# A two-layer decoder trunk on one core: squares, sums and transpositions of the feed-forward parts are placed anew, and the second output weights are prepared at another place

## The chip, the core and the metric

The kernel runs on one core of one Trainium2 chip. The core has five engines with instruction streams of their own: TensorE (PE, matrix products), VectorE (DVE), ScalarE (ACT), GpSimd (POOL) and SyncE (SP), which here only issues DMAs. Each engine works its stream off in order and waits where an operand of its next instruction is not ready. The metric is the device time of one execution in microseconds (us), the median of several runs.

## The reference

The input x is 1024 tokens by 1024 features, in float32. Two layers follow each other. A layer is a token mixer and a dense part, each with a residual and a LayerNorm:

```python
for i in range(DEPTH):                       # DEPTH = 2, ALPHA = 4 ** 0.25
    if i % 2 == 0:
        m = _mla(x, ...)                     # latent attention, 8 heads, ends in o @ w_o
    else:
        m = _diff_attn(x, ...)               # differential attention, 8 heads, RMS norm, ends in o @ w_o
    x = _layernorm(ALPHA * x + m, ln_mix_g[i], ln_mix_b[i])
    x = _layernorm(ALPHA * x + jnp.square(jax.nn.relu(x @ w_up)) @ w_down, ln_ffn_g[i], ln_ffn_b[i])
```

`w_up` is 1024 x 4096, `w_down` 4096 x 1024. Everything is float32, and the result is held to float32 closeness.

## The kernel before

**Numbers as pairs.** A float32 operand of a large product is scaled by a factor, cut into an upper and a lower float16 half, and multiplied in three float16 products (helper `mm3`, L185). ACT makes the upper half (L264), DVE the lower (L265). The factor comes from the root of a sum of squares: ACT squares rows with an accumulator, DVE sums (L269 turns the sum to bf16), PE adds over the partitions with a product of ones (L274, results called `tot_...`), and DVE and ACT make the root.

**Layers and names.** Names that end in A (or have A before a number) belong to the first layer, with B to the second. A layer runs in this order: mixer by heads, output projection `o @ w_o` with residual and LayerNorm by tiles of 128 tokens (`o_steps`: `scan` squares the rows of the o weights, `weights` halves them, `tile_steps` does a tile), the up projection, the down projection with the last LayerNorm. In the trace: latent attention 100 to 380 us, its output projection to 515, up A to 806, down A to 1128, a prologue of the differential attention to 1160, that attention to 1580, its output projection to 1705, up B to 1998, down B to the end at 2310.

**Up projection.** It goes by 16 groups g of features in a scheme of seven products for eight (`u_p1` to `u_p7`, 12 products of 128 x 512 each, into `ab`, `c`, `d`). ACT copies the first result out of PSUM with its scale into `pu` (L1039); this frees the PSUM tile `ab` for the products on `xT2`. The relu-squares go through GpSimd sums `hs` (L1094 to L1097) to a DRAM scratch `hs_d`. Beside it `wd_scan(g)` loads two 512 KB blocks of the down weights (`wds`, L1121, issued by SP) and squares them on ACT (L1122). The rows come from a ring of eight (tag `X`), which the results of the up projection share.

**Down projection.** Seven products m of eight steps st, 24 matrix products a step, on operands `h16` (read back from `hs_d` as `hr`) and `w16`, made by ACT and DVE some three steps ahead (`d_operands`). Its factors come from `down_scale`: key "A" for the first seven column sums, made in group 14; key "B" for all eight, made after step (0,2). At m = 5 the tiles 0 to 3 are finished (`fin_stats`, `fin_rstd`, `fin_apply`, L1229 to L250), and after m = 6 the tiles 4 to 7, tile by tile. In the first layer `to_xt` transposes each finished tile on PE (`tp_n`, L216) into the halves `xt_n`, on which the next layer's projections `qkv` run.

**Order.** Inside `in_order()` blocks (the up and down loops, the prologue of the differential attention) the engines follow the text of the program. Elsewhere a list scheduler moves instructions as buffers and operands allow. The fillers of an attention (`diff_filler`) hand it pieces of other work, each with a weight, to be put between score tiles. DMAs leave SP's queue in its order. The prologue re-reads tiles 6 and 7 of the first layer's result from DRAM (`x1_d`), transposes them and projects four token pairs of head 0 (`qkv0_0`, ...).

## Time and profile before

| what | value |
|---|---|
| median of 3 runs | 2301.41 us (2296.93 to 2302.53) |
| the profiled execution | 2311.53 us |
| its span in the trace | 2309.8 us |
| mean granted TensorE clock | 0.969 of full |
| PE busy | 2136.2 us, 92% of the span |
| DVE busy | 1684.8 us, 73% |
| ACT busy | 1300.7 us, 56% |
| POOL busy | 529.1 us, 23% |

The profiled execution is 10.1 us longer than the median of the runs that were only timed. A granted clock of 1 stands for 2.4 GHz, one of 0.5 for 1.2 GHz. PE's busy time counts slow products at their full length, so a stall costs its idle time and, where the clock falls behind it, half of the slow stretch as well.

### The profile page before, as it was taken

The page shows a single profiled execution, that of the slowest core. Times are in us where ns is not written, and L with a number is a line of the kernel's source. Part 1 is how long each engine was busy: PE and PEld are TensorE (multiplying, and loading weights), DVE is VectorE, ACT ScalarE, POOL GpSimd, SP SyncE. Part 2 cuts the span into 40 slices and gives each one's busy share as a digit, 9 for nine tenths or more (in the row PEclk, how much of TensorE's full clock was granted, in tenths as well). Part 3 has the DMA queues.
Part 4 walks back from the last instruction along what each step waited for, and adds up shares of the span by engine and source line. Part 5 has one row for each costly group of instructions (what it writes and reads, how often), then busy time and mean ns, then how long its engine had stood idle before and what let it go on. Part 6 is the DMA issues. An engine that isn't in the chain of part 4 may idle for free. (4 is left out here: it accounts for less than half of the span.)

```text
span 2309.8 us, 31741 instructions
## 1 busy us (share of the span) xinstructions
PE 2136.2 (92%) x11255; PEld 1191.6 (52%) x11255; DVE 1684.8 (73%) x2951; ACT 1300.7 (56%) x2400; POOL 529.1 (23%) x381
## 2 busy tenths in 40 slices
PE   7999898989999899999699999969989999999997
PEld 7878775444444344444356655644444444444443
DVE  5677675767777579877578888784857776588787
ACT  5465664446666355446388777673455665354443
POOL 1101001816666310000000001000826666300000
PEclk9999999989999999999899999988989999999999
DMA  4154767526666776652565565455436666856641
GB/s 146 33 104 91 147 123 188 194 101 205 207 213 207 264 281 218 201 192 82 160 155 126 126 122 106 84 118 150 162 142 205 209 210 223 326 198 210 218 155 55
DMA packets 454831, 384.29 MB, mean 166 GB/s; under 512 B 251376, under 2 KB 346624, under 8 KB 454672
## 3 DMA queue, kind: packets, MB, share of 16 engines
q1 hardware_dynamic: 452736, 376.51, 55.2%
q0 software_dynamic: 1936, 5.75, 0.9%
q8 instruction: 88, 1.44, 0.3%
q14 instruction: 71, 0.58, 0.1%
HBM read 247.97 MB, written 83.89 MB: 144 GB/s over the span
## 5 line engine op out<-in xcount | busy, mean ns | idle before, releaser
L185 PE MATMUL yA<-w16A,h16A 128*128 128x512 f16 x1344 | 294.9, 382 | 4.4 <-DVE X2A L1229 3.1
L185 PE MATMUL yB<-w16B,h16B 128*128 128x512 f16 x1344 | 292.8, 380 | 4.6 <-DVE X2B L1229 3.1
L185 PE MATMUL qkv<-wqkv,xt_nA 128*128 128x384 f16 x1536 | 268.5, 328 | 1.0 <-DVE wqkv L265 0.7
L185 PEld LDWEIGHTS <-wuB 128*128 128x128 f16 x1344 | 132.1, 99 | 172.0 <-issue 18.1
L185 PEld LDWEIGHTS <-wuA 128*128 128x128 f16 x1344 | 132.2, 99 | 170.9 <-issue 16.0
L185 PEld LDWEIGHTS <-h16A 128*128 128x128 f16 x1344 | 132.2, 98 | 167.3 <-issue 12.5
L185 PEld LDWEIGHTS <-h16B 128*128 128x128 f16 x1344 | 131.8, 98 | 168.1 <-issue 11.4
L185 PEld LDWEIGHTS <-xt_nA 128*128 128x128 f16 x1536 | 150.0, 99 | 95.8 <-issue 4.4
L1585 DVE TENSOR_REDUCE nmx_d<-ds 128x2 f32<-128x256 f32 (+5 forms) x96 | 90.1, 951 | 24.0 <-PE ds L413 23.6
L265 DVE SCALAR_TENSOR_TENSOR h16B<-hrB,SCB,h16B 128x1024 f16<-128x1024 f32 x56 | 73.3, 1308 | 37.8 <-ACT h16B L264 37.2
L265 DVE SCALAR_TENSOR_TENSOR h16A<-hrA,SCA,h16A 128x1024 f16<-128x1024 f32 x56 | 73.8, 1317 | 35.5 <-ACT h16A L264 35.4
L264 ACT ACTIVATE h16A<-hrA,SCA 128x1024 f16<-128x1024 f32 x56 | 63.9, 1141 | 61.0 <-issue 47.9
L264 ACT ACTIVATE h16B<-hrB,SCB 128x1024 f16<-128x1024 f32 x56 | 63.9, 1140 | 59.9 <-issue 47.9
L413 PE MATMUL s<-kn,qn 128*128 128x512 f32 (+2 forms) x288 | 83.5, 385 | 8.3 <-DVE ph L427 7.8
L185 PE MATMUL oA<-woA,otA 128*128 128x512 f16 x384 | 86.7, 387 | 4.1 <-DVE ph L427 4.1
L185 PE MATMUL oB<-woB,otB 128*128 128x512 f16 x384 | 85.4, 379 | 0.0
L265 DVE SCALAR_TENSOR_TENSOR wuB<-wuB_s,cuB,wuB 128x1024 f16<-128x1024 f32 (+1 forms) x32 | 56.7, 1771 | 34.9 <-ACT wuB L264 34.9
L185 PE MATMUL av_d<-pt16d,dv 128*128 128x256 f16 (+1 forms) x480 | 59.3, 277 | 24.4 <-DMA pt16d<-phd 24.4
L265 DVE SCALAR_TENSOR_TENSOR wuA<-wuA_s,cuA,wuA 128x1024 f16<-128x1024 f32 (+1 forms) x32 | 54.9, 1716 | 34.9 <-ACT wuA L264 34.9
L264 ACT ACTIVATE w16B<-wdB,RBB 128x1024 f16<-128x1024 f32 x40 | 45.7, 1142 | 53.5 <-DVE wdB L1186 53.5
L264 ACT ACTIVATE w16A<-wdA,RBA 128x1024 f16<-128x1024 f32 x40 | 45.7, 1141 | 53.4 <-DVE wdA L1186 53.4
L1489 POOL MEMSET ones_f<- 128x128 f32 x1 | 0.2, 205 | 305.3 <-PE yA L185 305.3
(876 smaller groups left out, 5099.1 us busy)
## 6 DMA issues: line engine op xcount, KB each, us to landing
hrA<-hs_d SPq DMA_DIRECT2D x56, 512.0 KB, 3.8
hrB<-hs_d SPq DMA_DIRECT2D x56, 512.0 KB, 3.8
wuA_r<-in_ffn_w_up_dram SPq DMA_DIRECT2D x32, 512.0 KB, 4.5
wdsA<-in_ffn_w_down_dram SPq DMA_DIRECT2D x32, 512.0 KB, 6.5
wdA<-in_ffn_w_down_dram SPq DMA_DIRECT2D x32, 512.0 KB, 4.7
wuB_r<-in_ffn_w_up_dram SPq DMA_DIRECT2D x32, 512.0 KB, 4.3
wdsB<-in_ffn_w_down_dram SPq DMA_DIRECT2D x32, 512.0 KB, 5.9
wdB<-in_ffn_w_down_dram SPq DMA_DIRECT2D x32, 512.0 KB, 4.6
```

What stands on the lines that cost most here:

```text
L185: nc.tensor.matmul(dst, l, r, start=first and m == 0, stop=last and m == n - 1, skip_group_check=resumed)
L264: nc.scalar.mul(hi, src, scale)
L265: nc.vector.scalar_tensor_tensor(out=lo, in0=src, scalar=scale, in1=hi, op0=ALU.mult, op1=ALU.subtract)
L413: nc.tensor.matmul(dst, q_, k_(c0 // 512, n), start=m == 0, stop=m == len(pairs) - 1)
L1489: nc.gpsimd.memset(ones_f, 1.0)
L1585: nc.vector.tensor_reduce(out=nmx[:, ms], in_=st["wide"][:, :, :nk] if i < 4 else st[m], axis=AX.X, op=ALU.max, negate=True)
```

## The change

Six things change.

1. The residual is no longer multiplied by ALPHA. The eight GpSimd multiplications a layer in `tile_steps` (L320) and the eight ACT multiplications a layer at step (0,4) of the down projection go. In their place the factor that the product is scaled back with is divided by ALPHA, and the LayerNorm's epsilon by ALPHA squared.
2. The end of `tile_steps` becomes three pieces (sums, squares, root).
3. `wd_scan` is cut in two. `wd_fetch(g + 1)` issues the loads at the start of iteration g, where load and squares stood before; `wd_scan(g + 1)`, now the squares alone, stands after `u_p5(g + 1)`.
4. `down_scale` is cut in two. `down_sum` (DVE's sum and its bf16 copy) stands earlier: before `u_p1` of group 14's iteration, and after step (0,0). `down_scale` keeps the product of ones and the root.
5. In the first layer tiles 0 to 3 are transposed one or two steps later, and tiles 6 and 7 straight from SBUF after their `fin_apply`, not from `x1_d` in the prologue.
6. The second layer's o weights: the text places the squares among the projections of head 6 (`H - 2`) in place of head 7, and part of the halves among head 7's.

```diff
@@ o_steps
             nc.vector.reciprocal(icw, cw)
+            nc.vector.tensor_scalar(out=icw, in0=icw, scalar1=1.0 / ALPHA, scalar2=None, op0=ALU.mult)
...
-                nc.gpsimd.tensor_scalar(out=t["x"], in0=t["x"], scalar1=ALPHA, scalar2=None, op0=ALU.mult)
...
-            def end():
-                nmean = residual(t["y"], icw, t["x"], f"m{nm}{i}")
-                st[i] = t["x"], nmean, ln_stats(t["x"], nmean, t["y"], f"m{nm}{i}")
+            def sums():
+                t["m"] = residual(t["y"], icw, t["x"], f"m{nm}{i}")
+            def squares():
+                t["q"] = ln_ssq(t["x"], t["m"], t["y"], f"m{nm}{i}")
+            def root():
+                st[i] = t["x"], t["m"], rstd_of(t["q"], 1.0 / D, LN_EPS_A, f"ln_m{nm}{i}")
@@ mixer_out_and_ffn
+            def wd_fetch(g):
+                wds[g] = [row(f"wds{nm}{g}{f_}") for f_ in range(2)]
+                for f_ in range(2):
+                    nc.sync.dma_start(out=wds[g][f_], in_=wdn[:, g, f_, :])
             def wd_scan(g):
-                for f_ in range(2):
-                    wr = row(f"wds{nm}{g}{f_}")
-                    nc.sync.dma_start(out=wr, in_=wdn[:, g, f_, :])
+                for f_, wr in enumerate(wds.pop(g)):
                     nc.scalar.activation(wr, wr, AF.Square, accum_out=wdsq[g // 2][...])
...
+            def down_sum(n, key):
+                tsum = fp.tile([P, 1], F32, tag="tsum", name=f"tsum{nm}{key}", bufs=2)
+                nc.vector.tensor_reduce(out=tsum, in_=c1["T"][:, :n], axis=AX.X, op=ALU.add)
+                tb[key] = total_in(tsum, f"cd{nm}{key}")
...
                     if g + 1 < NG:
-                        wd_scan(g + 1)
+                        wd_fetch(g + 1)
+                    if g == NG - 2:
+                        down_sum(NA, "A")
...
                         u_p5(g + 1)
+                        wd_scan(g + 1)
...
-                    if (m, st_) == (0, 4):
-                        for i in range(NT):
-                            nc.scalar.mul(X[i], X[i], ALPHA)
...
+                    if (m, st_) == (0, 0):
+                        down_sum(NS, "B")
                     if (m, st_) == (0, 2):
                         down_scale(NS, "B")
...
-                            if layer == 0 and i > 0:
+                        else:
+                            if layer == 0 and i in (1, 2):
                                 to_xt(xt_n, i - 1, "n", ps_wide)
-                        else:
                             fin_rstd(i)
                             fin_apply(i)
-                    if m == 6 and st_ == 1 and layer == 0:
-                        to_xt(xt_n, 3, "n")
+                    if m == 6 and st_ in (1, 2) and layer == 0:
+                        to_xt(xt_n, 1 + st_, "n")
...
+                if layer == 0:
+                    to_xt(xt_n, 6, "n")
                 fin_apply(7)
+                if layer == 0:
+                    to_xt(xt_n, 7, "n")
@@ diff_filler and prologue
+            if (h, u) in ((H - 2, 0), (H - 2, 2)):
+                steps = merge(steps, [(0.1, lambda k=k: wo_scan(k)) for k in range(2 * u, 2 * u + 4)])
+            if (h, u) == (H - 2, 3):
+                steps.append((0.1, wo_scale))
             if h == H - 1:
-                steps += [(0.1, lambda k=k: wo_scan(k)) for k in range(4 * u, 4 * u + 4)]
+                steps = merge(steps, [(0.1, lambda k=k: wo_load(k)) for k in range(2 * u, 2 * u + 2)])
...
-            xn = [wp.tile([P, D], F32, tag="raw", name=f"x1_{t}", bufs=3) for t in range(2)]
-            for t in range(2):
-                nc.gpsimd.dma_start(out=xn[t], in_=x1_d[(6 + t) * P : (7 + t) * P, :])
```

Four places show how the instructions move. The first is ScalarE in the second layer's up projection, between group 3's last piece and group 4's copy `puB4`; `wdsB40` and `wdsB41` are the two blocks of group 4, `wdsB30` and `wdsB31` those of group 3. Before:

```order
L264 ACTIVATE wuB4_3_16723<-wuB4_s4_16543,cuB4_16651 128x512
L1048 ACTIVATE hB30_16738<-abB1_16219,cuB3_16492 128x512
L1122 ACTIVATE wdsB40_16770,wdsqB4_16769<-wdsB40_16770 128x1024
L1122 ACTIVATE wdsB41_16773,wdsqB4_16769<-wdsB41_16773 128x1024
L1039 ACTIVATE puB4_16790<-abB0_16189,cuB4_16651 128x512
```

Now:

```order
L265 ACTIVATE wuB4_3_16697<-wuB4_s4_16516,cuB4_16625 128x512
L1057 ACTIVATE hB30_16712<-abB1_16195,cuB3_16465 128x512
L1136 ACTIVATE wdsB30_16590,wdsqB2_16566<-wdsB30_16590 128x1024
L1136 ACTIVATE wdsB31_16591,wdsqB2_16566<-wdsB31_16591 128x1024
L1048 ACTIVATE puB4_16763<-abB0_16165,cuB4_16625 128x512
```

The squares keep their place in the stream ahead of `pu`, but they are those of the group before, whose blocks were asked for one iteration earlier.

The second is TensorE after the first layer's last down product: `tp_nA50` to `tp_nA71` are the transpositions of the halves of tiles 5 to 7, and `qkv0_2` is the third projection block of head 0. Before (`x1_0` is the tile re-read from DRAM; tile 7 stands behind `qkv0_2`):

```order
L216 MATMUL tp_nA50_10117<-ident_r_77,X2A5_7920 128x128 x4
L216 MATMUL tp_nA51_10124<-ident_r_77,X2A5_7920 128x128 x4
L216 MATMUL tp_nA60_10260<-ident_r_77,x1_0_10178 128x128 x4
L216 MATMUL tp_nA61_10267<-ident_r_77,x1_0_10178 128x128 x4
L185 LDWEIGHTS xt_nA00_9498
L185 MATMUL qkv0_2_10274<-wqkv00_9846,xt_nA00_9498 128x384
```

Now:

```order
L217 MATMUL tp_nA50_10104<-ident_r_77,X2A5_7918 128x128 x4
L217 MATMUL tp_nA51_10111<-ident_r_77,X2A5_7918 128x128 x4
L217 MATMUL tp_nA60_10139<-ident_r_77,X2A6_7920 128x128 x4
L217 MATMUL tp_nA61_10146<-ident_r_77,X2A6_7920 128x128 x4
L217 MATMUL tp_nA70_10156<-ident_r_77,X2A7_7922 128x128 x4
L217 MATMUL tp_nA71_10163<-ident_r_77,X2A7_7922 128x128 x4
L186 LDWEIGHTS xt_nA00_9520
L186 MATMUL qkv0_2_10271<-wqkv00_9819,xt_nA00_9520 128x384
```

Tiles 6 and 7 come from the tiles `X2A6` and `X2A7` themselves, and both stand ahead of `qkv0_2`.

The third is ScalarE at the end of m = 5 and the start of m = 6 of the first layer's down projection; `woB...s_raw` are the squares of the second layer's o weights. Before, none of them stands here:

```order
L264 ACTIVATE h16A57_9588<-hrA57_9514,SCA_4631 128x1024
L264 ACTIVATE w16A57_9589<-wdA57_9516,RBA_4633 128x1024
L1248 ACTIVATE ljA2_9597,fsq_A2_9596<-X2A2_7914,rsum_fA2_9594 128x1024
L264 ACTIVATE xt_nA00_9498<-tp_nA10_9599,xs_c_1526 128x4x128
L264 ACTIVATE xt_nA01_9499<-tp_nA11_9606,xs_c_1526 128x4x128
L264 ACTIVATE h16A60_9639<-hrA60_9561,SCA_4631 128x1024
L264 ACTIVATE w16A60_9640<-wrA110_8034,RBA_4633 128x1024
```

Now:

```order
L265 ACTIVATE h16A57_9575<-hrA57_9485,SCA_4630 128x1024
L296 ACTIVATE woB1s_raw_14272,fwB_10172<-woB1s_raw_14272,gsub_1521 128x1024
L296 ACTIVATE woB2s_raw_14322,fwB_10172<-woB2s_raw_14322,gsub_1521 128x1024
L265 ACTIVATE w16A57_9576<-wdA57_9487,RBA_4632 128x1024
L296 ACTIVATE woB3s_raw_14339,fwB_10172<-woB3s_raw_14339,gsub_1521 128x1024
L1270 ACTIVATE ljA2_9584,fsq_A2_9583<-X2A2_7912,rsum_fA2_9581 128x1024
L265 ACTIVATE h16A60_9612<-hrA60_9548,SCA_4630 128x1024
L265 ACTIVATE w16A60_9613<-wrA110_8029,RBA_4632 128x1024
L265 ACTIVATE xt_nA00_9520<-tp_nA10_9618,xs_c_1526 128x4x128
L265 ACTIVATE xt_nA01_9521<-tp_nA11_9625,xs_c_1526 128x4x128
L296 ACTIVATE woB4s_raw_14547,fwB_10172<-woB4s_raw_14547,gsub_1521 128x1024
```

All eight squares lie between the halves of steps (5,6) and (6,2): the re-read tiles no longer hold two of the three buffers that the squares need, and the scheduler moves them up to where these are free. Before, they stood in the prologue.

The fourth is ScalarE in the last head. `woB0` to `woB3` are upper halves of o weights, `p_d7_1` and `phd7_0` pieces of the last head's score tiles, `phd6_7` one of the head before. Before:

```order
L1540 CAST dz7_6_15054<-qk7_6_14950 128x2x4x64
L264 ACTIVATE woB0_15134<-woB0w_raw_15132,fwB_10157 128x1024
L264 ACTIVATE woB1_15146<-woB1w_raw_15144,fwB_10157 128x1024
L264 ACTIVATE woB2_15170<-woB2w_raw_15168,fwB_10157 128x1024
L1588 ACTIVATE nmx_d7_1_14754<-nmx_d7_1_14754,w_c_4624 128x2
L426 ACTIVATE phd7_0_14730<-p_d7_0_14713,rec_d7_0_14725 128x128
L1590 ACTIVATE p_d7_1_14756,sume_d7_1_14755<-ds7_1_14757,nmx_d7_1_14754,w_c_4624 128x256
L1590 ACTIVATE ds7_1_14757,sume_d7_1_14755<-ds7_1_14757,nmx_d7_1_14754,w_c_4624 128x256
L264 ACTIVATE woB3_15175<-woB3w_raw_15173,fwB_10157 128x1024
```

Now:

```order
L1619 ACTIVATE ds6_6_1_14591,sume_d6_6_14551<-ds6_6_1_14591,nmx_d6_6_14550,w_c_4623 128x896
L265 ACTIVATE woB0_14876<-woB0w_raw_14874,fwB_10172 128x1024
L265 ACTIVATE woB1_14964<-woB1w_raw_14962,fwB_10172 128x1024
L265 ACTIVATE woB2_14999<-woB2w_raw_14997,fwB_10172 128x1024
L1617 ACTIVATE nmx_d6_7_14620<-nmx_d6_7_14620,w_c_4623 128x1
L1543 ACTIVATE qk7_6_14985<-qkv7_6_14903 128x256
L1569 CAST dz7_4_14847<-qk7_4_14790 128x2x4x64
L1545 ACTIVATE dv7_14476<-qkv7_6_14903 128x128
L1619 ACTIVATE p_d6_7_14622,sume_d6_7_14621<-ds6_7_0_14623,nmx_d6_7_14620,w_c_4623 128x1024
```

The halves now begin at score tile 6 of head 6 and lie beside the last projections (`qkv7_6`, `qkv7_7`); the last two of them stand beside head 7's first and shortest tile, and none behind it.

## Rows read from the trace of the kernel before

**Rows 1.** The span in stretches; columns in the first line, PEclk the granted clock.

```profile
core 0: us, PE busy (x) PEld busy (x) DVE busy (x) ACT busy (x) POOL busy (x), PEclk, DMA share, GB/s
1128.00:1160.00 32.00, 18.12 (x108) 11.61 (x107) 16.50 (x35) 16.02 (x35) 1.11 (x2) 0.73 0.72 218
1705.00:1998.00 293.00, 281.91 (x1298) 126.95 (x1296) 202.65 (x294) 172.25 (x280) 175.43 (x110) 0.99 0.64 218
```

**Rows 2.** Waits of TensorE over the span: total us, times, longest.

```profile
PE abA L185 <- ACT puA L1039: 8.7, 6, 4.4
PE abB L185 <- ACT puB L1039: 8.3, 5, 4.5
PE tot_cdBB L274 <- DVE totb_cdBB L269: 2.8, 1, 2.8
PE tp_nA L216 <- DMA x<-x_d: 13.9, 1, 13.9
PE tp_nA L216 <- DVE X2A L250: 5.7, 3, 3.0
PE ds L413 <- ACT woB L264: 4.5, 1, 4.5
```

**Rows 3.** Waits of TensorE, second layer's up projections, 1705 to 1998 us.

```profile
PE tot_cdBA L274 <- DVE totb_cdBA L269: 1.2, 1, 1.2
```

**Rows 4.** ScalarE in order of time: start, length, line, work, [idle before, releaser].

```profile
1763.12 1.06 ACT L1122 ACTIVATE wdsB<-wdsB 128x1024 f32<-128x1024 f32 x1 [1.64 <-issue]
1764.18 0.67 ACT L1039 ACTIVATE puB<-abB,cuB 128x512 f32<-128x512 f32 x1
```

**Rows 5.** TensorE in order of time, the same group; columns as in rows 4.

```profile
1764.90 4.33 PE L185 MATMUL abB<-xT2B,wuB 128*128 128x512 f16 x12 [1.91 <-ACT puB L1039]
```

**Rows 6.** The second layer's square rows, from issue to landing.

```profile
DMA to landing us min/median/max: 3.6/5.9/8.7
```

**Rows 7.** Stretches behind stalls; columns as in rows 1.

```profile
762.40:769.20 6.80, 5.98 (x15) 2.13 (x15) 2.45 (x5) 4.28 (x8) 0.00 (x0) 0.50 0.54 202
1765.90:1769.30 3.40, 3.40 (x10) 1.22 (x8) 2.40 (x2) 3.40 (x4) 1.79 (x2) 0.50 0.31 119
827.20:830.60 3.40, 3.40 (x10) 1.20 (x9) 1.72 (x4) 1.97 (x2) 0.00 (x0) 0.51 1.05 413
```

**Rows 8.** TensorE in order of time, end of the first down projection.

```profile
1098.34 7.31 PE L185 MATMUL qkv<-wqkv,xt_nA 128*128 128x384 f16 x44 [0.73 <-DVE wqkv L265]
1142.28 1.94 PE L216 MATMUL tp_nA<-ident_r,x 128*128 128x128 f32 x8 [13.88 <-DMA x<-x_d]
1144.01 6.08 PE L185 MATMUL qkv<-wqkv,xt_nA 128*128 128x384 f16 x24
```

**Rows 9.** VectorE in order of time, the same stretch.

```profile
1094.26 1.28 DVE L265 SCALAR_TENSOR_TENSOR w16A<-wrA,RBA,w16A 128x1024 f16<-128x1024 f32 x1
1128.71 1.41 DVE L265 SCALAR_TENSOR_TENSOR xt_nA<-tp_nA,xs_c,xt_nA 128x512 f16<-128x512 f32 x2 [2.74 <-ACT xt_nA L264]
1136.62 1.28 DVE L250 SCALAR_TENSOR_TENSOR X2A<-X2A,r_ln_fA,lnfbA 128x1024 f32<-128x1024 f32 x1
```

**Rows 10.** ScalarE in order of time, the second layer's o weights.

```profile
1149.68 1.15 ACT L295 ACTIVATE woB1s_raw<-woB1s_raw,gsub 128x1024 f32<-128x1024 f32 x1 [3.62 <-DMA woB1s_raw<-in_diff_w_o_dram]
...
1539.94 1.15 ACT L264 ACTIVATE woB<-woB3w_raw,fwB 128x1024 f16<-128x1024 f32 x1 [4.43 <-DMA woB3w_raw<-in_diff_w_o_dram]
```

**Rows 11.** The last head's tail; columns as in rows 1.

```profile
1525.00:1578.00 53.00, 28.14 (x125) 15.79 (x124) 40.08 (x82) 37.13 (x80) 0.00 (x0) 0.65 0.54 128
```

**Rows 12.** VectorE's groups, 380 to 515 us: busy us, mean ns, idle before.

```profile
L247 DVE SCALAR_TENSOR_TENSOR XA<-XA,rsum_mA,lnmgA 128x1024 f32<-128x1024 f32 x6 | 10.6, 1770 | 0.0
L230 DVE SCALAR_TENSOR_TENSOR XA<-oA,fwA,XA 128x1024 f32<-128x1024 f32 x6 | 7.7, 1278 | 7.2 <-POOL XA L320 6.5 <-PE oA L185 0.8
L247 DVE SCALAR_TENSOR_TENSOR XA<-x_early,rsum_mA,lnmgA 128x1024 f32<-128x1024 f32 x2 | 2.5, 1276 | 0.0
```

**Rows 13.** Waits of SyncE's DMA queue, 1705 to 1998 us.

```profile
SPq L1121 <- ACT wdsB L1122: 5.4, 1, 5.4
```

More of the change, by code (lines that the diff above doesn't have):

```diff
@@ L141, in consts @@
         return t
+    LN_EPS_A = LN_EPS / ALPHA ** 2
     eps_t = consts("eps_t", [LN_EPS, RMS_EPS])
@@ L234, in residual, with ln_ssq @@
         return n
-    def ln_stats(xrow, nmean, junk, nm):
+    def ln_ssq(xrow, nmean, junk, nm):
         ssq = sm.tile([P, 1], F32, tag="lnsq", name=f"lnsq_{nm}", bufs=3)
         nc.scalar.activation(junk, xrow, AF.Square, bias=nmean, accum_out=ssq)
-        return rstd_of(ssq, 1.0 / D, LN_EPS, f"ln_{nm}")
+        return ssq
     def ln_apply(dst, xrow, nmean, r, g, b, done=None):
@@ L332, in products @@
                     )
-            def end():
-                nmean = residual(t["y"], icw, t["x"], f"m{nm}{i}")
-                st[i] = t["x"], nmean, ln_stats(t["x"], nmean, t["y"], f"m{nm}{i}")
-            return [(0.1, start)] + [(1.3, lambda k=k: products(k)) for k in range(H)] + [(0.1, end)]
+            def sums():
[4 more added lines that the diff above has]
+                st[i] = t["x"], t["m"], rstd_of(t["q"], 1.0 / D, LN_EPS_A, f"ln_m{nm}{i}")
+            return (
+                [(0.1, start)]
+                + [(1.3, lambda k=k: products(k)) for k in range(H)]
+                + [(0.1, sums), (0.1, squares), (0.1, root)]
+            )
         return scan, scale, weights, tile_steps, st
@@ L1113, in u_out @@
                     )
+            wds = {}
+            def wd_fetch(g):
+                wds[g] = [row(f"wds{nm}{g}{f_}") for f_ in range(2)]
+                for f_ in range(2):
+                    nc.sync.dma_start(out=wds[g][f_], in_=wdn[:, g, f_, :])
             def wd_scan(g):
@@ L1118, in wd_scan, with down_scale @@
                     wdsq[g // 2] = fp.tile([P, 4], F32, tag="wdsq", name=f"wdsq{nm}{g}", bufs=3)
-                for f_ in range(2):
-                    wr = row(f"wds{nm}{g}{f_}")
-                    nc.sync.dma_start(out=wr, in_=wdn[:, g, f_, :])
+                for f_, wr in enumerate(wds.pop(g)):
                     nc.scalar.activation(wr, wr, AF.Square, accum_out=wdsq[g // 2][:, 2 * (g % 2) + f_ : 2 * (g % 2) + f_ + 1])
-            def down_scale(n, key):
+            tb = {}
+            def down_sum(n, key):
                 tsum = fp.tile([P, 1], F32, tag="tsum", name=f"tsum{nm}{key}", bufs=2)
                 nc.vector.tensor_reduce(out=tsum, in_=c1["T"][:, :n], axis=AX.X, op=ALU.add)
-                inv_root(c1["cd" + key], total(tsum, f"cd{nm}{key}", ps_mm if key == "A" else ps_wide), 1.05 * D_SPREAD / F16_TOP ** 2)
-                nc.vector.reciprocal(c1["icd" + key][:, 0:1], c1["cd" + key])
-                nc.vector.tensor_scalar(
-                    out=c1["icd" + key][:, 1:2], in0=c1["icd" + key][:, 0:1], scalar1=-1.0, scalar2=None, op0=ALU.mult
-                )
+                tb[key] = total_in(tsum, f"cd{nm}{key}")
+            def down_scale(n, key):
+                pn = total_out(tb[key], f"cd{nm}{key}", ps_mm if key == "A" else ps_wide)
+                inv_root(c1["cd" + key], pn, 1.05 * D_SPREAD / F16_TOP ** 2)
+                icd = c1["icd" + key]
+                nc.vector.reciprocal(icd[:, 1:2], c1["cd" + key])
+                for n_, sign in ((0, 1.0 / ALPHA), (1, -1.0 / ALPHA)):
+                    nc.vector.tensor_scalar(
+                        out=icd[:, n_ : n_ + 1], in0=icd[:, 1:2], scalar1=sign, scalar2=None, op0=ALU.mult
+                    )
                 nc.vector.tensor_scalar(
@@ L1252, in fin_rstd @@
                 nmean, ssq = fin[i]
[L1253 removed]
+                fin[i] = nmean, rstd_of(ssq, 1.0 / D, LN_EPS_A, f"ln_f{nm}{i}")
             def fin_apply(i):
@@ L1310, in mixer_out_and_ffn @@
                         to_xc(key, src, i - 4)
+            wd_fetch(0)
             wd_scan(0)
@@ L1661, in last_filler @@
             if u == 2:
-                return [(0.1, wo_scale)] + [(0.1, lambda k=k: wo_load(k)) for k in range(H)]
+                return [(0.1, lambda k=k: wo_load(k)) for k in range(4, H)]
             def x_t(i):
```

3 lines of the change are left out of this document (removed).

## The prediction

> **What bounds the kernel now.** I read the stretches first. In the second layer's up projection TensorE is busy 281.9 of 293 us and the next engine 202.7 [rows 1], so TensorE bounds it, and what can be won there is its own idle time and its slow clock; the first layer's up projection is built alike. Next I read TensorE's waits by what ended them [rows 2]. Two of the largest sums are the waits of the `ab` products for ScalarE's copy `pu`: 8.7 us in six waits and 8.3 us in five. The single longest is a transposition that waits 13.9 us for a tile re-read from DRAM. Then I followed one `pu` wait in order of time: ScalarE idles 1.64 us ahead of the second square of `wds`, works 1.06 us on it, and only then makes `puB`, 0.67 us [rows 4]; TensorE has idled 1.91 us when it goes on [rows 5]. The idle time has no releaser in the row, but the block that it squares takes 3.6 to 8.7 us from issue to landing [rows 6], so I read it as the block's arrival. Last I looked at the clock behind such a wait: for 6.8 and for 3.4 us it is 0.50, the 1.2 GHz level [rows 7], so the same products take longer too.
>
> **The squares of the up projection (part 3).** The order on ScalarE keeps two squares ahead of `pu`, but they now read blocks that were asked for a whole group earlier. The latest landing of 8.7 us [rows 6] is far shorter than a group: sixteen groups in 293 us [rows 1] are some 18 us each. So the idle time ahead of the squares goes. What is late next is the scale chain and `hB`, which already stand at these places in the groups without a wait. Won: 8.7 + 8.3 = 17.0 us of waits. Behind them lie one slow stretch of 6.8 us in the first layer and two like the one of 3.4 us in the second; at half the clock half of each is lost: 3.4 + 1.7 + 1.7 = 6.8 us. Together 23.8; I take 24. Bounds: 17 if the clock falls for other reasons, 26 with small slips of a few tenths that the rows put to others. At the end the squares of group 15 (two of 1.06 us) fall ahead of the first down operands; ScalarE has idle time there, so nothing.
>
> **The sums of the down projection (part 4).** The two early sums cost a wait of 1.2 us each, one in each layer [rows 3], the late ones 2.8 each [rows 2], the first layer having its like. VectorE's sum now stands several operands earlier, so the product of ones finds it ready: 1.2 + 1.2 + 2.8 + 2.8 = 8.0. Behind the late one the clock is 0.51 for 3.4 us [rows 7], in each layer: 2 x 1.7 = 3.4. Of 11.4 I take 10, because without the wait the steps behind come sooner to operands that read DRAM scratch back. Bounds 6 and 11.4.
>
> **Removed multiplications (parts 1 and 2).** ScalarE's sixteen at step (0,4) lie where operands are ahead: nothing, and if that cover were gone at most a wait of some us. GpSimd's sixteen show once: VectorE's residual in the first layer waits 6.5 us for them [rows 12]. But TensorE does not wait for that residual in any row of size. Six of VectorE's rows there take 1.770 us on the mean, against 1.276 for the two of the same work that ran before them [rows 12]: 3.0 us a layer that can come back. Bounds 0 and +6 for both layers; I take 2, near the lower end.
>
> The Trainium skill, "SBUF — State Buffer", section "Who interferes with whom", says that a VectorE instruction with two inputs in SBUF contends with a GpSimd instruction that reads SBUF. The two means agree with it. By it the whole 6 us should come back, and the sum would be 4 us better.
>
> **End of the first down projection (parts 5 and 6).** The 5.7 us of waits for `X2A` at m = 5 go, since the transpositions stand one or two steps later [rows 2]. But what ends this stretch is not TensorE: before the projections of head 0 it waits for the halved `wqkv` (0.73 us [rows 8]), and VectorE makes these right behind the last operand, `w16A67`, at 1094.26 [rows 9]. ScalarE now has the eight squares of the o weights among these operands, 8 x (1.15 + 0.19) = 10.7 us, some 1.3 each by [rows 10]. Following the new order by hand with these durations, VectorE idles for ScalarE two to four us at three places, and `w16A67` comes about 2.6 us later. So the 5.7 us pass over to a wait for `wqkv`, and I count -2.6 there.
>
> The wait of 13.9 us for the re-read tile [rows 2, 8] goes as such. But `qkv0_2` now has the transpositions of tiles 6 and 7 ahead of it. Tile 7 is ready when its last row ends, 1136.62 + 1.28 = 1137.9 [rows 9]. VectorE now also has tile 6's two lower halves ahead of that row, 1.41 us like those at 1128.71 [rows 9]: 1139.3. Then come the transposition of tile 7 and its halves, and behind them on VectorE the pieces of `qkv0_0` that free the PSUM tile for `qkv0_2`; from transposition to product it was 1.73 us before [rows 8], with VectorE's 1.41 about 3, and a little for the pieces: some 1143 to 1144, against 1144.01 before. The wait changes its name and is nearly as long. Won: 0 to 5 us if the chain is shorter; I take 0.6, as only tile 7's transposition behind `qkv0_2` goes for sure. With -2.6 this makes -2. Bounds -6 (each of the squares waiting for its block, as one did for 3.62 us [rows 10], beyond its cover) and +14 (the old wait gone whole).
>
> **The last head (part 6).** Between 1525 and 1578 us TensorE is busy 28.1 of 53 us at a clock of 0.65 [rows 11]; ScalarE works 37.1, VectorE 40.1. A score tile waits 4.5 us behind halves of o weights on ScalarE [rows 2], and ScalarE itself 4.43 us for a block of them [rows 10]. The halves (8 of some 1.15 us on ScalarE, as many on VectorE) now lie beside the last projections, where TensorE has products of its own. Upper bound: all 8 x 1.15 = 9.2 us and the 4.4 of waiting, 13.6, so +14. Lower bound -2: the last projections wait for them instead. I take +6, between, as the later tiles wait for their softmax and not for the halves. The rest of both attentions moves little; 0 within 2.
>
> **Sum.** 24 + 10 + 2 - 2 + 6 = 40 us. The profiled execution would go from 2311.5 to 2271.5 us. It lay 10.1 us above the median of the runs, 2301.4, so I predict 2301.4 - 40, about 2262 us. The likeliest case's own range, with some bounds on either side at once, is 2250 to 2278.
>
> **Rivals.**
> - *The wait for `pu` stays (18%).* The waiting squares may not be what makes `pu` late: 1.64 us has no releaser [rows 4], and the group before them may end later when nothing holds TensorE back. Against it: the wait of TensorE, 1.91, is close to ScalarE's idle time. Then part 3 gives some 5 of 24: 40 - 19 = 21, 2280 us.
> - *The prologue's wait goes whole (10%).* If the pieces of `qkv0_0` do not hold `qkv0_2`, the 13.9 us go, with part of the slow clock that makes TensorE's mean 0.73 from 1128 to 1160 [rows 1]: 13 more, 2249 us. Against it: tile 7's own end at 1137.9 alone leaves 9.5 of it.
> - *Slower: the ring of eight rows (7%).* The fetch now holds two of the eight rows for a whole group longer. SyncE's queue has waited at this very issue for the squares of an earlier block, once, 5.4 us [rows 13]. If that comes in each group, the store of `hB`, the three stores of `hs` and the next loads of up weights wait behind it, and TensorE with them where a load's lead is used up. From 1.5 us a group in 28 groups the 40 us are lost; at 2.5 us the time is 2262 + 70 = 2332. Against it: a group's lead is 18 us, and the order shows the fetch in the same place of the queue.
> - The squares of the o weights holding up the operands of m = 6 is in the bounds above; alone it can't turn the sign.
>
> **How the numbers follow.** The forecast has 62%, the rivals 18, 10 and 7, and 3% are left for gains that cancel. About 0.3%, 7 us, is what a measurement of this kernel can tell from no change. Forecast, the first two rivals and their mixtures are all faster by more, less a few per cent of the first: 0.87. Slower: the third rival and half of the rest, 0.08. Same: 0.05. Range: the upper end takes in the first rival with the lower bounds of others, 2288; the lower end the second with the full 26 of part 3, 2244.
>
> **What would show it.** Right: no wait of `ab` for `pu` over half a microsecond in either layer, and both up stretches 10 to 13 us shorter; no wait for `totb_cd`; the clock at 1 behind both places. The prologue: a wait of `qkv0_2` for VectorE in place of the one for `x`. The last head's tail some 6 us shorter, without a wait for `woB`. Wrong: waits for `pu` of the old size with ScalarE never idle ahead of the squares; waits of SyncE at the fetch; or waits of the `y` products for `w16A` at m = 5 and 6 of more than the 2.6 us counted.

## The result and the profile after

| | before | after |
|---|---|---|
| median, four runs each on one chip | 2301.97 us (2296.93 to 2305.86) | 2272.01 us (2267.8 to 2272.7) |
| ratio, 95% interval | | 0.9867 [0.9844, 0.989] |
| the profiled execution | 2311.53 us | 2272.7 us |
| its span | 2309.8 us | 2270.9 us |

The change saves 30.0 us by the medians and 38.8 us between the two profiled executions. 2262 us was predicted, with a range of 2244 to 2288.

I cut both spans at TensorE's instructions, by the first or last product of a name (`oA`, `dA`, `yA`, ...). The stretches where something moves, in us:

| stretch of TensorE's rows | before | after |
|---|---|---|
| last `oA` to first `dA` (end of the first output projection) | 44.5 | 40.5 |
| first `dA` to first `yA` (up A); the same for B | 285.0; 285.9 | 274.0; 274.0 |
| first 192 `yA` products; the same for B | 47.4; 47.4 | 42.7; 42.7 |
| `yA` products of m = 5; of m = 6 and the rest | 50.4; 57.3 | 43.2; 67.9 |
| last `yA` to `qkv0_2`; the projections behind it | 16.9; 11.0 | 17.0; 9.9 |
| head 7's last projections; from there to its last `ds` | 23.9; 53.3 | 22.3; 50.6 |
| last `av_d` to last `oB`; to first `dB` | 66.3; 40.4 | 72.4; 32.1 |

The first view of the kernel after is that of the stretches, with the columns of [rows 1]: the prologue, up B, the places that answer to the three of [rows 7], and the last head's tail [rows 11].

```profile
1112.20:1144.20 32.00, 20.10 (x114) 12.78 (x113) 17.99 (x41) 11.60 (x30) 1.16 (x4) 0.73 0.27 81
1682.80:1963.90 281.10, 278.25 (x1298) 125.47 (x1297) 204.39 (x295) 170.21 (x280) 180.99 (x110) 1.00 0.67 227
1741.00:1744.40 3.40, 3.40 (x18) 1.52 (x16) 2.02 (x8) 1.66 (x4) 3.32 (x4) 1.00 0.55 212
752.10:758.90 6.80, 6.59 (x32) 2.95 (x31) 5.42 (x11) 4.07 (x6) 3.16 (x3) 1.00 0.93 330
809.70:813.10 3.40, 3.40 (x17) 1.52 (x16) 2.02 (x7) 1.86 (x4) 0.00 (x0) 1.00 1.04 416
1507.00:1560.00 53.00, 29.07 (x148) 16.76 (x147) 39.83 (x76) 35.61 (x79) 0.00 (x0) 0.74 0.58 132
```

Up B is 12 us shorter while TensorE's busy time falls by 3.7 us only: mostly idle time went. The clock is 1.00 in each place that had been at 0.50 or 0.51. The prologue's clock is 0.73 as before.

TensorE's waits that answer to [rows 2] or are new at the same places:

```profile
PE av_d L186 <- DMA pt16d<-phd: 17.8, 14, 4.2
PE ds L423 <- DVE p_d L1632: 14.8, 4, 7.8
PE tp_nA L217 <- DVE y_ln_fA L160: 6.0, 1, 6.0
PE qkv L186 <- DVE dv L1546: 4.5, 3, 2.2
PE tp_nA L217 <- DVE X2A L251: 4.2, 1, 4.2
PE tp_nA L217 <- DVE xt_nA L266: 3.9, 1, 3.9
PE yA L186 <- DVE w16A L266: 2.7, 1, 2.7
PE abA L186 <- ACT hA L1057: 1.1, 2, 0.6
```

No wait for `pu` is left, and none for `totb_cd`; of `ab`, 1.1 us of waiting for `hA` remains in the first layer, and as much for `hB` in the second. Waits for `X2A`, for the re-read tile and for `woB` stood in [rows 2]; in their places stand the waits of `tp_nA` for tiles 6 and 7, one of `yA` for `w16A`, and those of the last score tiles for `p_d`.

The group of [rows 4] on ScalarE, and TensorE beside it as in [rows 5]:

```profile
1736.97 0.67 ACT L1057 ACTIVATE hB<-abB,cuB 128x512 f32<-128x512 f32 x1
1737.54 1.04 ACT L1136 ACTIVATE wdsB<-wdsB 128x1024 f32<-128x1024 f32 x1
...
1738.58 1.04 ACT L1136 ACTIVATE wdsB<-wdsB 128x1024 f32<-128x1024 f32 x1
...
1739.61 0.67 ACT L1048 ACTIVATE puB<-abB,cuB 128x512 f32<-128x512 f32 x1
```

```profile
1737.92 2.75 PE L186 MATMUL abB<-xT3B,wuB 128*128 128x512 f16 x12
1740.64 0.17 PE L275 MATMUL tot_wuB<-totb_wuB,ones_b 128*128 128x2 bf16 x1
1740.67 2.75 PE L186 MATMUL abB<-xT2B,wuB 128*128 128x512 f16 x12
```

Neither square has idle time in brackets, `pu` ends at 1740.28, and TensorE's product on `xT2B` starts with no wait. Twelve such products take 2.75 us, where [rows 5] has 4.33.

At the end of the first down projection TensorE shows, in order of time, what came in place of [rows 8]:

```profile
1052.28 6.81 PE L186 MATMUL yA<-w16A,h16A 128*128 128x512 f16 x23 [2.71 <-DVE w16A L266]
...
1069.00 1.97 PE L217 MATMUL tp_nA<-ident_r,X2A 128*128 128x128 f32 x8 [3.85 <-DVE xt_nA L266]
...
1084.22 7.31 PE L186 MATMUL qkv<-wqkv,xt_nA 128*128 128x384 f16 x44 [0.73 <-DVE wqkv L266]
...
1118.56 1.94 PE L217 MATMUL tp_nA<-ident_r,X2A 128*128 128x128 f32 x8 [5.97 <-DVE y_ln_fA L160]
...
1124.66 1.94 PE L217 MATMUL tp_nA<-ident_r,X2A 128*128 128x128 f32 x8 [4.17 <-DVE X2A L251]
...
1128.37 9.75 PE L186 MATMUL qkv<-wqkv,xt_nA 128*128 128x384 f16 x48 [1.76 <-DVE dv L1546]
```

The first three rows lie in m = 6. Behind the last `yA`, one wait of 13.88 us has become three, of 5.97, 4.17 and 1.76 us, and `qkv0_2` starts as long after the last `yA` as before.

### The profile page after: what moved, and what is told of

Its sections match the earlier page's. It is cut to its first block, busy times and chain, and to the rows that moved or that the text cites. A ratio compares the mean times of both kernels' runs of the same rounds, so it can differ in the third digit from the quotient of the medians.

```text
span 2270.9 us, 31756 instructions
## 1 busy us (share of the span) xinstructions
PE 2127.6 (94%) x11255; PEld 1189.7 (52%) x11255; DVE 1678.9 (74%) x2957; ACT 1279.8 (56%) x2384; POOL 488.2 (21%) x363
## 5 line engine op out<-in xcount | busy, mean ns | idle before, releaser
L186 PEld LDWEIGHTS <-xt_nA 128*128 128x128 f16 x1536 | 150.5, 99 | 102.2 <-issue 11.2
L1614 DVE TENSOR_REDUCE nmx_d<-ds 128x2 f32<-128x256 f32 (+5 forms) x96 | 90.1, 953 | 20.4 <-PE ds L423 19.8
L265 ACT ACTIVATE w16B<-wdB,RBB 128x1024 f16<-128x1024 f32 x40 | 45.7, 1142 | 52.4 <-DVE wdB L1208 52.4
```

The lines of the kernel that those rows point to most:

```text
L186: nc.tensor.matmul(dst, l, r, start=first and m == 0, stop=last and m == n - 1, skip_group_check=resumed)
L265: nc.scalar.mul(hi, src, scale)
L1614: nc.vector.tensor_reduce(out=nmx[:, ms], in_=st["wide"][:, :, :nk] if i < 4 else st[m], axis=AX.X, op=ALU.max, negate=True)
```

## The experiments

Differences are between medians, and are against the kernel after (2272.01 us) unless said otherwise. A row called "before" is the unchanged kernel before on the same chip. Intervals are of the ratio to that. The medians of "before" lie between 2301.48 and 2304.56 us, so a difference from the kernel after, which had another "before" beside it, can be some 3 us off. The nine timed runs of the kernel after (four, and five in experiment 9) lie between 2267.7 and 2275.7 us. All runs of experiments 3, 4, 8 and 10 lie above that; differences of some 5 us and less are not separated.

### 1. The kernel before, profiled a second time

No edit. The forecast took its waits from one profiled execution, which had taken 10 us more than the median.

> The kernel before, unchanged, for a second profile of it. Open is that the two profiled executions lie 38.8 us apart and the medians only 30. Theory A (the waits for pu, which hang on when blocks land, were longer in the one profiled execution): the up stretches of this profile are some 280 to 283 us instead of 285.0 and 285.9, its time about 2302, the rest of the stages within 1 us of the first profile. Theory B (the difference lies in attention or the output projections): the up stretches stay at 285 and 286 within 1 us and another stage is 5 to 10 us shorter. Timed against before: ratio 1.000 within 0.002.

Measured: 2303.34 us, ratio 1.0004 [0.9991, 1.0016]; the profiled execution took 2305.2, its span 2303.4. TensorE's waits for `pu`, to be laid beside [rows 2]:

```profile
PE abA L185 <- ACT puA L1039: 7.8, 6, 4.0
PE abB L185 <- ACT puB L1039: 3.4, 5, 1.5
```

The same eleven waits add up to 11.2 us, not 17.0, and the up stretches are 282.7 and 278.7, not 285.0 and 285.9. So the two stretches were 9.5 us longer in the first profile. The first execution was 6.4 us longer in all; the other stretches of the second are 3.1 us longer, as its first output projection begins at 385.6 us in place of 382.0.

### 2. The fetch ahead alone

The kernel before with part 3 of the change (`wd_fetch` as there) and nothing else.

```diff
...
+            wd_fetch(0)
-                        wd_scan(g + 1)
+                        wd_fetch(g + 1)
...
                         u_p5(g + 1)
+                        wd_scan(g + 1)
```

> The kernel before with part 3 alone (blocks of the down weights asked for one iteration ahead of their squares). Main theory: the waits of ab for pu go, both up stretches become 274 to 275.5 us; against the medians 17 to 24 us faster (ratio 0.990 to 0.9925). Rival (the squares are not what makes pu late): waits for pu stay over 8 us in sum, under 8 us faster.

Measured: 2290.82 us, 0.9942 [0.9927, 0.9956], 13.2 us below before (2304.02). No wait for `pu` is left; up A and up B take 275.3 each. The gain is real, and smaller than the 24 of the forecast and the 17 expected here.

### 3. The change without the fetch ahead

```diff
                         wd_fetch(g + 1)
+                        wd_scan(g + 1)
...
                         u_p5(g + 1)
-                        wd_scan(g + 1)
```

> The changed kernel with part 3 taken back (load and squares at the old place, the squares right behind the load's issue). Main theory: waits for pu of 14 to 18 us come back in the two up stretches, 282 to 286 us each; 16 to 24 us slower than the changed kernel, about 2288 to 2296 us. Rival: within 8 us of the changed kernel.

Measured: 2285.88 us, 0.9912 [0.9892, 0.9932], 13.9 us more than after. The up stretches are 281.8 and 283.1. TensorE's waits, and ScalarE's groups of squares (total idle time ahead of them is behind the second bar, then its releasers):

```profile
PE abB L186 <- ACT puB L1048: 7.3, 4, 4.0
PE abA L186 <- ACT puA L1048: 6.6, 5, 3.9
```

```profile
L1136 ACT ACTIVATE wdsA<-wdsA 128x1024 f32<-128x1024 f32 x32 | 33.7, 1054 | 16.2 <-issue 6.0 <-POOL hsA12a L1105 4.2 <-DMA wdsA<-in_ffn_w_down_dram 1.7
L1136 ACT ACTIVATE wdsB<-wdsB 128x1024 f32<-128x1024 f32 x32 | 33.7, 1053 | 14.2 <-issue 6.0 <-POOL hsB12a L1105 4.1 <-DMA wdsB<-in_ffn_w_down_dram 1.9
```

The same groups in the kernel after:

```profile
L1136 ACT ACTIVATE wdsA<-wdsA 128x1024 f32<-128x1024 f32 x32 | 33.4, 1044 | 1.4 <-issue 1.3
L1136 ACT ACTIVATE wdsB<-wdsB 128x1024 f32<-128x1024 f32 x32 | 33.3, 1044 | 1.4 <-DMA wdsB<-in_ffn_w_down_dram 1.4
```

The releasers named there (issue, GpSimd) hide the cause, and the landing times in the trace show it: of the 28 squares of the kernel before that had over 0.3 us of idle time ahead of them, 27 begin 0.02 to 0.10 us after their own block has landed; here it is 24 of 26. The place of the square alone puts the idle time back, 30.4 us on ScalarE against 2.8, and 13.9 us (7.3 and 6.6) of TensorE's waits. Given back, it costs less than the 16 to 24 us expected here. Taken alone (13.2) or given back (13.9; 11.8 if each kernel is set against its own "before"), part 3 is worth the same within what these runs can tell, so no overlap with the other parts shows.

### 4. The sums late again

```diff
             def down_scale(n, key):
+                down_sum(n, key)
...
-                    if g == NG - 2:
-                        down_sum(NA, "A")
...
-                    if (m, st_) == (0, 0):
-                        down_sum(NS, "B")
```

> The changed kernel with part 4 taken back (the sum of the down projection's squares made at the place of its root). Main theory: the waits for totb_cd return, 2 x 1.2 and 2 x 2.8 us, and with the slow clock behind them 8 to 11.4 us in all: 2280 to 2283 us, the first 192 products of each down projection take 47 us instead of 42.7. Rival (the steps behind wait for their operands anyway): under 4 us slower.

Measured: 2280.88 us, 0.9896 [0.988, 0.9912], 8.9 us more. TensorE's waits of before are back to the tenth [rows 2, 3], the first layer's among them:

```profile
PE tot_cdAB L275 <- DVE totb_cdAB L270: 2.8, 1, 2.8
PE tot_cdBB L275 <- DVE totb_cdBB L270: 2.8, 1, 2.8
...
PE tot_cdAA L275 <- DVE totb_cdAA L270: 1.2, 1, 1.2
PE tot_cdBA L275 <- DVE totb_cdBA L270: 1.2, 1, 1.2
```

The first 192 `y` products take 45.7 us in the first layer and 47.4 in the second, against 42.7: 3.0 and 4.7 us. The stretches right behind the two late waits tell why they differ:

```profile
813.50:816.90 3.40, 3.40 (x17) 1.56 (x16) 1.89 (x5) 1.78 (x2) 0.00 (x0) 1.00 1.05 411
1985.40:1988.80 3.40, 3.40 (x10) 1.30 (x9) 1.90 (x5) 1.50 (x2) 0.00 (x0) 0.55 1.04 408
```

After the same 2.8 us of idle time the clock stayed at 1.00 in one layer and was 0.55 in the other. The wait costs its own length; what the clock adds is not the same each time.

### 5. Tiles 6 and 7 re-read in the prologue

```diff
-                if layer == 0:
-                    to_xt(xt_n, 6, "n")
                 fin_apply(7)
-                if layer == 0:
-                    to_xt(xt_n, 7, "n")
...
+            xn = [wp.tile([P, D], F32, tag="raw", name=f"x1_{t}", bufs=3) for t in range(2)]
+            for t in range(2):
+                nc.gpsimd.dma_start(out=xn[t], in_=x1_d[(6 + t) * P : (7 + t) * P, :])
...
+                if t in (1, 2):
+                    transpose_in16(xn[t - 1], xt1[1], t + 1, f"nA{5 + t}", sx[:, 2:3])
```

With the re-read tiles holding two buffers, the scheduler also puts the eight squares back into the prologue.

> The changed kernel with tiles 6 and 7 re-read from DRAM in the prologue again and transposed there; the re-read tiles hold two of three buffers, so the squares of the o weights stand in the prologue again too. Main theory (the changed tail has swapped one wait for others, and the squares hold up m = 6): from the last down product to the second block of head 0 it is 17 us as before and as now, a wait of about 13.9 us for the re-read tile is back in place of waits of 6.0, 4.2 and 1.8 us, and m = 6 gets 3 to 7 us shorter since the wait of 2.7 us for w16A goes: 2266 to 2270 us. Rival (the new tail is worth the removed wait): 5 us slower or more, above 2277.

Measured: 2266.85 us, 0.9837 [0.9805, 0.987], 5.2 us less than after. The long wait is back,

```profile
PE tp_nA L217 <- DMA x<-x_d: 14.2, 1, 14.2
```

and yet the tail from the last `yA` to `qkv0_2` is 17.2 us against 17.0: nothing was won there by keeping the tiles in SBUF. What is shorter is m = 6, 63.1 us against 67.9; the attention (349.0 against 346.9) and the last projections (24.3 against 22.3) give 4 of it back in this profile.

### 6. Only the eight squares back in the prologue

```diff
-            if (h, u) in ((H - 2, 0), (H - 2, 2)):
-                steps = merge(steps, [(0.1, lambda k=k: wo_scan(k)) for k in range(2 * u, 2 * u + 4)])
...
+                if t == 3:
+                    for k in range(H):
+                        wo_scan(k)
```

> The changed kernel with the eight squares of the second o weights placed behind the last projection of the prologue, tail as changed. Main theory (the squares hold up the operands of m = 6): the wait of the y products for w16A (2.7 us) goes, m = 6 is 3 to 7 us shorter than 67.9 us, the tail's 17 us stay; head 0 takes up to 4 us back: 2266 to 2271 us. Rival (VectorE alone bounds m = 6): m = 6 stays within 1 us of 67.9 and the kernel within 3 us of the changed one or slower.

Measured: 2268.09 us, 0.9841 [0.981, 0.9871], 3.9 us less. m = 6 takes 61.6 us, the wait of `yA` for `w16A` of 2.7 us is gone, and the tail is 17.0. So it is the squares among the operands that lengthen m = 6, by 6.3 us: it takes 66.8 to 70.4 us in the eight profiles that have them there, and 61.6 to 63.1 in the three of the changed kernel that don't. Both this and experiment 5 point to a faster kernel; neither interval excludes no difference from after.

### 7. The halves back in the last head

```diff
-            if (h, u) == (H - 2, 3):
-                steps.append((0.1, wo_scale))
-            if h == H - 1:
-                steps = merge(steps, [(0.1, lambda k=k: wo_load(k)) for k in range(2 * u, 2 * u + 2)])
...
-                return [(0.1, lambda k=k: wo_load(k)) for k in range(4, H)]
+                return [(0.1, wo_scale)] + [(0.1, lambda k=k: wo_load(k)) for k in range(H)]
```

> The changed kernel with the halves of the second o weights, and their factor, among the last head's tiles again. Main theory (the halves' place is worth what the two profiles show, 1.6 + 2.7 us): 2 to 6 us slower, 2274 to 2278 us, a wait of ds for woB on ScalarE of some 4.5 us is back. Rival (the place is worth the 6 us forecast or more): 7 us slower or more. Second rival: no difference, within 1.5 us.

Measured: 2274.62 us, 0.9866 [0.9835, 0.9896], 2.6 us more than after. The wait of 4.5 us is back, behind the same three halves of `woB` and under another name:

```profile
PE ds L423 <- ACT nmx_d L1617: 4.5, 1, 4.5
```

But the waits for `p_d` on VectorE are 11.3 us in place of 14.8, and the stretch to the last `ds` is 50.8 against 50.6. Only the last projections differ, 23.9 against 22.3. Against its own "before" this kernel saves 29.9 us, as much as the kernel after with 30.0. The halves' move is worth 0 to 3 us, and these runs don't separate it from nothing.

### 8. The halves earlier still

```diff
-            if (h, u) == (H - 2, 3):
+            if (h, u) == (H - 2, 2):
                 steps.append((0.1, wo_scale))
-            if h == H - 1:
-                steps = merge(steps, [(0.1, lambda k=k: wo_load(k)) for k in range(2 * u, 2 * u + 2)])
+            if (h, u) == (H - 2, 3):
+                steps = merge(steps, [(0.1, lambda k=k: wo_load(k)) for k in range(4)])
```

> The changed kernel with the factor made behind head 6's third and the first four halves with its fourth stretch of filler, so that all eight lie beside score tiles 4 to 6 of head 6. If the new wait of 7.8 us of the last head's first score tile for VectorE comes from the halves queued ahead of it, it shrinks to under 5 us and the kernel is 2 to 7 us faster, 2265 to 2270. If the tail is bound by softmax and transposing DMAs alone, within 2 us of the changed kernel.

Measured: 2278.66 us, 0.989 [0.9854, 0.9925], 6.6 us more. TensorE's waits from 1480 to 1600 us:

```profile
PE av_d L186 <- DMA pt16d<-phd: 14.2, 4, 4.5
PE ds L423 <- DVE p_d L1632: 8.8, 2, 6.0
```

In the kernel after, that stretch has 4.2 us in one wait for `pt16d` and 14.1 in three for `p_d`. The wait for the softmax became smaller, and waits for transposed tiles that come by DMA became larger; the stretch to the last `ds` grew from 50.6 to 58.5 us. Neither expectation came true: the longest such wait is 6.0 us and not under 5, and the kernel became slower. One of the eight halves on ScalarE begins behind the last projections here, where it is four in the kernel after; fewer of them there do not by themselves shorten the last head.

### 9. The kernel after, again

No edit.

> The changed kernel once more, for its spread on the chip of these runs: 2268 to 2274 us, both up stretches 273.3 to 274.5 us, since nothing there waits for a landing block any more; against before 0.985 to 0.989.

Measured: 2272.89 us, 0.9853 [0.9829, 0.9877]. Up A and up B 273.3 and 273.4 (after 274.0 both).

### 10. GpSimd's multiplications back

```diff
-            nc.vector.tensor_scalar(out=icw, in0=icw, scalar1=1.0 / ALPHA, scalar2=None, op0=ALU.mult)
...
+                nc.gpsimd.tensor_scalar(out=t["x"], in0=t["x"], scalar1=ALPHA, scalar2=None, op0=ALU.mult)
...
-                st[i] = t["x"], t["m"], rstd_of(t["q"], 1.0 / D, LN_EPS_A, f"ln_m{nm}{i}")
+                st[i] = t["x"], t["m"], rstd_of(t["q"], 1.0 / D, LN_EPS, f"ln_m{nm}{i}")
```

> The changed kernel with GpSimd's sixteen multiplications of the residual back (the factor and epsilon of that LayerNorm as before). The output projections and what lies up to the first d product take 138.6 us in the changed kernel's profile for the first layer's 94.0 + 40.5 and the second's 72.4 + 32.1 us (239.0 in all), 246.1 before. Theory A (GpSimd's multiplications make VectorE's rows beside them longer and the residual late): 4 to 8 us of it come back, 2275 to 2280 us. Theory B (the three pieces of the tile's end moved the transpositions): within 2 us of the changed kernel.

Measured: 2280.56 us, 0.9895 [0.9874, 0.9916], 7.7 us more than experiment 9 on the same chip. VectorE's groups in the first output projection with the multiplications (columns as in [rows 12]), and then in the kernel after; `t_ln_mA` and `r_ln_mA` are short rows of the LayerNorm's root, one of each for a tile:

```profile
L248 DVE SCALAR_TENSOR_TENSOR XA<-XA,rsum_mA,lnmgA 128x1024 f32<-128x1024 f32 x6 | 10.4, 1727 | 0.0
L231 DVE SCALAR_TENSOR_TENSOR XA<-oA,fwA,XA 128x1024 f32<-128x1024 f32 x6 | 7.7, 1279 | 7.2 <-POOL XA L321 6.5 <-PE oA L186 0.7
L163 DVE SCALAR_TENSOR_TENSOR t_ln_mA<-r_ln_mA,y_ln_mA 128x1 f32<-128x1 f32 x8 | 6.4, 800 | 0.5 <-ACT r_ln_mA L162 0.5
L165 DVE TENSOR_TENSOR r_ln_mA<-r_ln_mA,t_ln_mA 128x1 f32<-128x1 f32 x8 | 4.8, 596 | 0.2
```

```profile
L248 DVE SCALAR_TENSOR_TENSOR XA<-XA,rsum_mA,lnmgA 128x1024 f32<-128x1024 f32 x6 | 9.5, 1579 | 0.0
L231 DVE SCALAR_TENSOR_TENSOR XA<-oA,fwA,XA 128x1024 f32<-128x1024 f32 x6 | 7.7, 1277 | 4.7 <-PE oA L186 4.7
L248 DVE SCALAR_TENSOR_TENSOR XA<-x_early,rsum_mA,lnmgA 128x1024 f32<-128x1024 f32 x2 | 2.5, 1276 | 0.0
L163 DVE SCALAR_TENSOR_TENSOR t_ln_mA<-r_ln_mA,y_ln_mA 128x1 f32<-128x1 f32 x8 | 3.7, 462 | 0.5 <-ACT r_ln_mA L162 0.5
L165 DVE TENSOR_TENSOR r_ln_mA<-r_ln_mA,t_ln_mA 128x1 f32<-128x1 f32 x8 | 2.1, 263 | 0.2
```

The stretch from the last `oA` to the first `dA` is 43.7 us with the multiplications and 40.7 in experiment 9. This one is steady: 43.7 to 44.5 in the four profiles that have them, 40.4 to 40.7 in the ten that don't. In the second layer (last `av_d` to first `dB`) the figures are 106.6 to 107.2 and 100.3 to 107.9, so its share can't be read from single profiles; the means are 106.9 and 104.0. No run puts ScalarE's sixteen multiplications back alone. The second layer's first 192 `y` products, beside which they stood, take 47.4 us in the kernel before and 47.4 in experiment 4, which has late sums and no such multiplications, so no effect of them shows.

### 11 and 12. One piece for the end of a tile, and a version of both

Experiment 11 puts `sums`, `squares` and `root` back into one piece; experiment 12 is that together with experiment 6.

```diff
-                + [(0.1, sums), (0.1, squares), (0.1, root)]
+                + [(0.1, lambda: (sums(), squares(), root()))]
```

> The changed kernel with the tile's end (sums, squares, root) as one piece of filler again. Theory A (GpSimd is the cause of the gain in the output projections): within 2 us of the changed kernel, 2270 to 2274. Theory B (the three pieces are): 4 to 8 us slower, the first layer's stretch from the last o product to the first d product some 44 us again instead of 40.5.

Measured: 2271.59 us, 0.9856 [0.9833, 0.9878]: no difference that can be told.

> The changed kernel with the squares of the second o weights in the prologue and the tile's end in one piece. If both runs read rightly, m = 6 of the first layer is 61.6 us again instead of 67.9, the rest as in the changed kernel: 2264 to 2270 us, 4 to 8 us under the changed kernel, against before 0.982 to 0.986. If the shorter m = 6 is given back in head 0, within 2 us of the changed kernel.

Measured: 2269.9 us (2266.45 to 2273.49, six runs), 0.986 [0.9839, 0.988] to a before of 2301.48. m = 6 is 61.6 us again, but the stretch to the last `ds` is 54.1 against 50.6. It lies at the edge of what was expected and can't be told from the kernel after. No version here is shown to be faster than the change.

## Why the prediction came out as it did

The direction was right, the mechanisms of the two largest terms were right, and 2272.01 lies in the range. The forecast was 10 us too low. One step is as large as that. The other four terms miss by -1.1, +5.7, -1.9 and -3.4 us, and that they cancel to -0.7 is luck.

- **The conversion to the median, and the size of part 3.** Between the profiled executions 40 us were forecast, to 2271.5; it became 38.8, to 2272.7. The step that failed is "It lay 10.1 us above the median of the runs, 2301.4, so I predict 2301.4 - 40". It takes for granted that the extra 10 us lie outside the 40. Experiment 1 shows that the up stretches of that execution were 9.5 us longer than those of a second one, 5.8 of it in the waits that part 3 removes, and with them in slow products. Against the median part 3 is worth 13.2 (experiment 2) to 13.9 (experiment 3), not 24, and lies below the lower bound of 17. That bound was the sum of the waits of that one execution; a bound from a wait that varies has to come from more than one. The ends of the whole range don't follow from their own words either: the second rival with the full 26 of part 3 is 2249 - 2 = 2247, not 2244, and the first rival with all the others' lower bounds is 2280 + 4 + 2 + 4 + 8 = 2298, not 2288. The measured time lies far inside both.
- **Its mechanism** held. The idle time ahead of the squares went from 30.4 us to 2.8 by moving them alone (experiment 3), every `pu` wait went, and the clock behind it stayed at 1.00. That the squares waited for their blocks, read from [rows 4, 6] without a releaser, the landing times bear out (experiment 3). The rival that the wait for `pu` stays is excluded by both experiments.
- **The sums: 10 forecast, 8.9 measured** (experiment 4). The four waits were read right to the tenth. Of the slow clock, 3.4 us counted, only the second layer's came back when the sums were late.
- **Removed multiplications: 2 forecast, 7.7 measured** (experiment 10). This term was undersized, and its upper bound of 6 too low. "TensorE does not wait for that residual in any row of size" was true of the names in the rows, and not of the chain: TensorE waits in this stretch for transposed pieces that stand behind the residual. 3.0 us are steady in the first layer. The six rows of VectorE that the forecast priced gave back only 10.4 - 9.5 = 0.9 there, and the idle time ahead of the residual fell from 7.2 to 4.7, by 2.5. It passed over the sixteen short rows of the LayerNorm's root, which also read two inputs: 6.4 + 4.8 us with the multiplications and 3.7 + 2.1 without, 5.4 us less, and in the second layer 5.3 + 3.8 against 2.0 + 2.1. Six rows of `wuA` became longer, by 1.7. The Trainium skill's rule that VectorE's rows with two SBUF inputs contend with GpSimd's reads ("SBUF — State Buffer", section "Who interferes with whom") agrees with the direction: 1727 ns against 1579, and 1276 for the two early rows. The whole 6 us that the prediction worked out from it would have been nearer than the 2 it took. Which part sets TensorE's time is not shown; the order on GpSimd itself and the rows' speed weren't separated.
- **The squares and transpositions: -2 forecast.** By the stretches of the table it is 7.2 won in m = 5, 10.6 lost in m = 6, 0.1 lost and 1.1 won behind: -2.4. Undoing them gives -3.9 (experiment 6) to -5.2 (experiment 5). The forecast that the 13.9 us of [rows 8] change their name and stay as long came out: 17.0 us to `qkv0_2` against 16.9. But the 5.7 us of m = 5 did not pass over to a wait for `wqkv`, which is 0.73 us as before; they went in m = 6 itself. `w16A` was expected 2.6 us late, and TensorE's wait for it is 2.71, a tenth over the sign of being wrong. The whole effect of the squares on m = 6 is larger, 6.3 us: idle time of 2.7 for `w16A`, 0.2 and 0.9 more for transposed pieces, and for the rest slower products, as the clock falls. The stretch from 1049 to 1060 has 0.84 granted (the row below). The other 4.3 of the 10.6 stay without the squares (experiment 6); a transposition waits 3.0 us for `xt_nA` there, and no such wait stands in the kernel before.

```profile
1049.00:1060.00 11.00, 8.29 (x35) 3.85 (x34) 8.60 (x12) 4.30 (x7) 0.00 (x0) 0.84 0.58 190
```

- **The halves: +6 forecast, 2.6 measured** (experiment 7), not separated from nothing. The tail came out 2.7 us shorter and the last projections 1.6, but the tail stays as short with the halves put back. The wait for `woB` did go, but the score tiles behind it wait for `p_d` instead (14.8 us). "No wait for `woB`" was a poor sign to look for: the next wait in the same place takes up most of it.
- **The ring of eight rows.** Its sign came, and its harm did not. SyncE's queue waits at the fetch in both layers, where [rows 13] has one wait of 5.4 us:

```profile
SPq L1129 <- DVE hA L1039: 17.6, 12, 2.0
SPq L1129 <- DVE hB L1039: 17.6, 12, 2.0
SPq L1129 <- ACT junkA L949: 13.4, 1, 13.4
SPq L1129 <- ACT junkB L949: 13.4, 1, 13.4
```

  That is 31.0 us a layer: 13.4 once, at the first group, and up to 2.0 in twelve later ones, 2.1 on the mean of fifteen; the prediction put the turning point at 1.5 us a group. The releasers are the other users of the ring, not the squares of an earlier block as in [rows 13]. Experiment 2 has the same waits. TensorE has no wait for a load or a store in either up stretch, so what stands behind the fetch on SyncE must have had more lead than the wait took. The prediction priced a wait of the queue as a wait of TensorE, and that was wrong.

Undone one by one, the parts give 13.9 + 8.9 + 7.7 + 2.6 - 3.9 = 29.2 us, and the whole is 30.0. That agreement is partly luck, as each term is uncertain by some 3 us: with each kernel set against its own "before" the terms are 11.8, 6.8, 7.7, 0.0 and -6.5, together 19.8. So up to 10 us may lie in what the parts do together, and these runs don't tell.

Open are the lengths of the stretches that the list scheduler fills. Last `av_d` to first `dB` varies from 100.3 to 105.4 us between eight profiles of kernels that are alike there, and the stretch to the last `ds` from 48.8 to 54.6 between nine; I did not find what sets it.

## What to carry to other kernels

Before a sum from a profile is taken off a median, ask where the profiled execution's extra time lies; where it lies in the waits that the change removes, take the sum off the profiled time, or profile the kernel a second time. A load asked for one loop turn earlier took a data wait out of an in-order engine's path here, and the waits that it put on the issuing queue held up no product. A step that is put "where the engine is idle" among operands made just in time is not free: eight squares among such operands lengthened their stretch by 6 us. When a slow row is priced, look for short rows of the same kind beside it: sixteen of one element a partition gave back six times as much as the six long ones.
